# Moving a norm into a product and giving a 17th pair of columns to the seven-product scheme, in a hybrid decoder block

## The chip, the cores and the metric

The kernel runs on one core of a Trainium2 chip. The metric is the device time of one execution in microseconds (us). The core's engines are named as in the profile: PE (matrix products; PEld is its weight load), DVE (elementwise work), ACT (activations and copies), POOL and SP. POOL and SP do little here but issue DMA transfers.

## The reference, cut to what matters

The block adds 16 meta tokens to 512 tokens of width 1024, mixes them with two recurrent mixers and an output projection, and then applies a gated feed-forward part. The change touches the end of the output projection and the feed-forward part:

```
h = h + conv_glu_ffn(rmsnorm(h, norm2_w[l]), ffn_w_up[l], ffn_conv_w[l],
                     ffn_conv_b[l], ffn_w_down[l])

def conv_glu_ffn(h, w_up, conv_w, conv_b, w_down):
    u = causal_dwconv(h @ w_up, conv_w, conv_b)      # width 2 * 2816, 3 taps
    gate, val = jnp.split(u, 2, axis=-1)
    return (jax.nn.silu(gate) * val) @ w_down
```

Here rmsnorm multiplies each token by the reciprocal root of its mean square and each channel by norm2_w. A factor per token may be applied before or behind a product over the channels.

## The kernel before, in words

Tokens lie along the free axis, channels along the 128 partitions. A product of f32 accuracy is made of three passes over rounded halves: weight high with data high, weight high with data low, weight low with data high. Each weight chunk of 128 x 1024 is therefore loaded as a raw tile (SP), rounded to a high half (ACT, L182) and subtracted to a low half (DVE, L183). Raw tiles, high halves and low halves have three buffers each, so a split waits until PE has finished with the chunk three places earlier.

The up projection has 22 pairs of column blocks, j (gate) and 22 + j (value). KINDS gives the way of each pair.

- U: a plain product with u2, which is h times norm2_w without the factor per token; the result is multiplied by the factor rstd2 behind the product (tile fr, L963), and then the three taps are added up (L929 on ACT, two L931 on DVE). 48 matmuls a block, 96 a pair.
- N: the same product with the normed tokens n, which hold the factor already. There is no fr, and the taps read the product's bank.
- W: seven products of half size in place of eight (function scheme). The weights of three chunks are w0, w2 and w1 with a half chunk s4; sums of weight blocks for them are made in device memory by accumulating transfers that POOL issues (weight_sums, L209 to L217, in four groups, the last one gated by xr5 near the end of the output projection). The tokens are n and four sums t1 to t4 of quarter blocks of n. 84 matmuls a pair. Each pair also copies a partial result from one bank to another on ACT (L989) and takes s4 through a tile of its own (SP, then s4h on ACT, s4l on DVE).

The first five pairs of the up projection are U. In their time n and t are made, two of eight steps behind each pair: an even step of normed_tokens makes two n (L902) with their halves (L189, L190), an odd one the sums t with theirs (L912 to L915). Then come 16 W pairs and one N pair, and then the down projection, whose inputs ac (products of gate and value) have to be split as well; SPLITS says behind which pair each ac is split.

rstd2 is made by second_norm: two products of ones with the sum of squares (tiles psn2), a logarithm on ACT (L140) and an exponential (L141). ACT loads a table of functions where the next function is not in the one it holds.

The order on each engine is set when the program is built: a planner places the instructions of all engines by priorities and its own model of time, and issue_after ties an instruction behind another. Each engine, and the SP queue, then works strictly in that order. What stands behind a waiting instruction waits with it.

Of the kernel before, what the change touches and what calls it, by code (L numbers as in the profile page):

```python
# [10 lines left out]
AF = mybir.ActivationFunctionType  # L11
ALU = mybir.AluOpType
# [7 lines left out]
T0 = META - 2  # L20
NB = 4
DM = 1024
KD = DM // P
# [24 lines left out]

KINDS = "UUUUUWWWWWWWWWWWWWWWWN"
STEPS = {0: (0, 1), 1: (2, 3), 2: (4, 5), 3: (6, 7)}
SPLITS = {7: (0,), 8: (1, 2), 10: (3,), 13: (4,), 15: (5,), 18: (6,), 20: (7, 8), 21: range(9, 22)}
WS = [j for j in range(KF) if KINDS[j] == "W"]
GROUPS = WS[0:4], WS[4:8], WS[8:12], WS[12:]
HT = 258
# [6 lines left out]
def tile_block(ctx: ExitStack, tc: tile.TileContext, xT, w_in, w_dt, w_out, w_up, w_down,  # L63
               par, consts, consti, out, dbg=None):
    nc = tc.nc
    V, A, G, PE = nc.vector, nc.scalar, nc.gpsimd, nc.tensor
# [9 lines left out]
    def slot(name, n=NT, dtype=F32, parts=P, tag="m"):  # L76
        return gp.tile([parts, n], dtype, tag=tag, name=name, bufs=TAGS[tag])
# [35 lines left out]
    LOGS = "natural_log_exp_and_others"  # L113
# [78 lines left out]
    def weight_sums(js, behind):  # L192

        n = GROUPS.index(js)
        V.tensor_copy(ticks[:, n:n + 1], behind[:, T0:T0 + 1])
        gate = G.tensor_copy(tick[:], ticks[:, n:n + 1])
        halves = w_up.rearrange("(a j) p c -> j p a c", a=2)
        ds = {}
        for j in js:
            t = dp.tile([P, 4 * HK], F32, name=f"sums{j}")  # L200
            sumd[j] = t
            ds[j] = t[:].rearrange("p (n c) -> p n c", n=4)

        def twice(ap):
            return ap.unsqueeze(1).broadcast_to([P, 2, HK])

        with tc.issue_after(gate.ins):
            for j in js:
                G.dma_start(ds[j][:, 0:2], halves[j][:, :, 0:HK])  # L209
                G.dma_start(ds[j][:, 2:4], w_up[j].rearrange("p (n c) -> p n c", n=2))  # L210
            for j in js:
                G.dma_start(ds[j][:, 0:2], twice(w_up[KF + j][:, HK:]), accum_op=ALU.add)
                G.dma_start(ds[j][:, 2], w_up[KF + j][:, 0:HK], accum_op=ALU.add)
            for j in js:
                G.dma_start(ds[j][:, 0], w_up[KF + j][:, 0:HK], accum_op=ALU.add)
            for j in js:
                G.dma_start(ds[j][:, 3], ds[j][:, 0], accum_op=ALU.add)  # L217
# [42 lines left out]
        ahead(used[0] + 2)  # L260
        return wdone.pop(key)

    def product(groups, xh, xl, t0, nk, k0=0):


        for k in range(len(xh)):
            first, last = k0 + k == 0, k0 + k == nk - 1
            for ps, (hi, lo) in groups:
                wh, wl = hi[:, k * P:(k + 1) * P], lo[:, k * P:(k + 1) * P]
                for w, x, s, e in ((wh, xh[k], first, False), (wh, xl[k], False, False), (wl, xh[k], False, last)):  # L270
                    for a0, a1 in ((t0, HALF), (HALF, NT)):
                        PE.matmul(ps[:, O + a0:O + a1], w, x[:, a0:a1], start=s, stop=e)  # L272
# [29 lines left out]
    with first(190000):  # L302
# [3 lines left out]
        acc = None  # L306
# [538 lines left out]
    for j, s in oorder:  # L845
        w = weights("out", j, s)
        if s:
            pos[j] = banks2(f"pout{j}")
            product([(pos[j], w)], obh, obl, T0, 2 * KD)
            continue  # L850
        product([(pos[j], w)], oah, oal, T0, 2 * KD, KD)
        xr = slot(f"xr{j}", tag="y")
        nc.scalar.dma_start(xr[:, T0:], xT[:, j, T0:])
        V.tensor_tensor(xr[:, T0:], xr[:, T0:], pos[j][:, O + T0:O + NT], ALU.add)
        dump(f"h{j}", xr[:])
        hs.append(xr)
        if j == 5:
            weight_sums(GROUPS[3], xr)
        hi, lo = slot(f"u2h{j}", dtype=F32R, tag="u"), slot(f"u2l{j}", dtype=F32R, tag="u")
        A.activation(hi[:, T0:], xr[:, T0:], AF.Copy, scale=col(C_N2 + j))  # L860
        V.scalar_tensor_tensor(lo[:, T0:], xr[:, T0:], col(C_N2 + j), hi[:, T0:].bitcast(F32),
                               ALU.mult, ALU.subtract)
        u2h.append(hi)
        u2l.append(lo)
        sq = slot(f"hsq{j}", tag="pr")
        A.activation(sq[:, T0:], xr[:, T0:], AF.Square)
        if acc is None:
            acc = sq
        else:
            V.tensor_tensor(acc[:, T0:], acc[:, T0:], sq[:, T0:], ALU.add)  # L870
    rstd2 = slot("rstd2", tag="rs")

    u1 = []
# [75 lines left out]
    def conv3(j, kind):  # L949
        w = weights("up", j)  # L950
        ps = product_banks(False)[0]
        if kind == "U":
            product([(ps, w)], u2h, u2l, T0, KD)
        else:
            product([(ps, w)], nh, nl, T0, KD)
        if j == 0:
            second_norm()
        r = ps[:, O + T0:O + NT]
        c = slot(f"fc{j}", 512, tag="pr")
        with evac():  # L960
            if kind == "U":
                t = slot(f"fr{j}", tag="pr")
                V.tensor_tensor(t[:, T0:], r, rstd2[:, T0:], ALU.mult)  # L963
                r = t[:, T0:]
            taps(c[:], r, j, taps_of(j), col(C_FB + j))
        return c
# [214 lines left out]
```

## Time and profile before

| | |
|---|---|
| time, median of 3 runs | 872.89 us (872.69 to 874.68) |
| the profiled execution's own time | 873.16 us |
| span of its profile | 871.3 us |
| matmuls and DMA as the page counts them | PE x6746, 135.00 MB moved by DMA |
| output projection | to 501 us |
| five U pairs | 501 to 559 us |
| 16 W pairs | 559 to 728 us |
| N pair and down projection | to 862 us |

The three runs lie within 0.23% of each other. The profile's times count from the start of the span. The stage borders are read from PE's rows. Line numbers in the text are those of the kernel before; in the changed one, what stands from L272 on is two to five lines further down.

### The profile page before, as it was taken

How to read it: one execution, taken by the hardware profiler on the slowest of the kernel's cores; microseconds unless marked ns; L12 is line 12 of the kernel's file. 1: busy time of each engine (PE TensorE's matmuls, PEld its weight loads, DVE VectorE, ACT ScalarE, POOL GpSimd, SP SyncE). 2: the span in 40 equal slices, each digit the busy share in tenths (PEclk: the TensorE clock that was granted, in tenths of full speed). 3: DMA queues.
4: the chain of work that ended last, by engine and by line, in shares of the span. 5: the costliest groups of instructions: out<-in, count | busy, mean ns of one | idle time of the engine just before them, and what ended most of it. 6: DMA issues, size and time to landing. Idle time of an engine off the chain costs nothing.

```text
span 871.3 us, 16400 instructions
## 1 busy us (share of the span) xinstructions
PE 851.0 (98%) x6746; PEld 810.3 (93%) x6746; DVE 579.6 (67%) x970; ACT 464.1 (53%) x736; POOL 93.7 (11%) x130
## 2 busy tenths in 40 slices
PE   6999999999999999999999999999999999999995
PEld 6999899999999999999999999889999999888885
DVE  6984978799776766545333359978888886633233
ACT  8638975966445434454222265567666665533231
POOL 1000000003213221202221312100000000000001
PEclk9999999999999999999999999999999999999998
DMA  7234242213989598948998889756555553243312
GB/s 248 93 109 163 78 145 62 76 58 128 240 153 166 208 228 160 180 128 305 222 179 178 279 163 192 178 166 185 182 173 189 177 176 115 68 126 90 91 43 97
DMA packets 51867, 135.00 MB, mean 155 GB/s; under 512 B 5432, under 2 KB 9016, under 8 KB 51792
## 3 DMA queue, kind: packets, MB, share of 16 engines
q1 hardware_dynamic: 33392, 92.60, 33.1%
q0 software_dynamic: 15872, 37.75, 23.1%
q10 hardware_dynamic: 2528, 3.60, 1.3%
q8 instruction: 53, 0.87, 0.4%
q14 instruction: 22, 0.18, 0.1%
HBM read 131.78 MB, written 39.90 MB: 197 GB/s over the span
## 4 chain that ended last, share of the span: by engine, by line
PE 87%; DVE 6%; DMA 2%; ACT 2%; issue 1%; SPq 0%; DVEq 0%; ACTq 0%
PE pj L272 32%; PE pout L272 10%; PE pdn L1054 4%; PE pdn L1055 4%; PE pdn L1053 4%; PE pup L982 3%; PE pup L984 3%; PE pup L983 3%; PE psn L983 2%; PE psn L984 2%; PE psn L982 2%; PE pup L272 1%; DVE fc L931 1%; PE pdn L1068 1%; PE pdn L1067 1%
## 5 line engine op out<-in xcount | busy, mean ns | idle before, releaser
L272 PE MATMUL pj<-u_lo,whi_in 128*128 128x272 f32 (+1 forms) x752 | 156.5, 288 | 0.0
L272 PE MATMUL pj<-u_hi,wlo_in 128*128 128x272 f32 (+1 forms) x752 | 156.1, 286 | 0.0
L272 PE MATMUL pj<-u_hi,whi_in 128*128 128x272 f32 (+1 forms) x752 | 155.3, 287 | 0.0
L272 PEld LDWEIGHTS pj<-u_lo,whi_in 128*128 128x128 f32 x752 | 116.1, 188 | 2.4 <-issue 1.9
L272 PEld LDWEIGHTS pj<-u_hi,wlo_in 128*128 128x128 f32 x752 | 116.4, 189 | 2.0 <-issue 1.9
L272 PEld LDWEIGHTS pj<-u_hi,whi_in 128*128 128x128 f32 x752 | 115.6, 188 | 2.4 <-issue 2.3
L183 DVE TENSOR_TENSOR wlo_in<-raw_in,whi_in 128x1024 fp32r<-128x1024 f32 (+1 forms) x58 | 64.3, 1109 | 55.1 <-ACT whi_in L182 55.0
L182 ACT ACTIVATE whi_in<-raw_in 128x1024 fp32r<-128x1024 f32 (+1 forms) x58 | 56.1, 966 | 64.5 <-PE pj L272 59.2
L182 ACT ACTIVATE whi_w<-raw_w 128x1024 fp32r<-128x1024 f32 x48 | 50.7, 1056 | 22.8 <-PE pup L983 11.5
L183 DVE TENSOR_TENSOR wlo_dn<-raw_dn,whi_dn 128x1024 fp32r<-128x1024 f32 (+1 forms) x24 | 27.2, 1135 | 53.3 <-ACT whi_dn L182 53.3
L183 DVE TENSOR_TENSOR wlo_w<-raw_w,whi_w 128x1024 fp32r<-128x1024 f32 x48 | 58.6, 1221 | 5.5 <-ACT whi_w L182 5.0
L182 ACT ACTIVATE whi_dn<-raw_dn 128x1024 fp32r<-128x1024 f32 (+1 forms) x24 | 23.6, 989 | 69.2 <-PE pdn L1054 53.6
L1054 PE MATMUL pdn<-ac_lo,whi_dn 128*128 128x512 f32 (+1 forms) x154 | 55.9, 363 | 0.0
L1053 PE MATMUL pdn<-ac_hi,whi_dn 128*128 128x512 f32 (+1 forms) x154 | 55.7, 362 | 0.0
L1055 PE MATMUL pdn<-ac_hi,wlo_dn 128*128 128x512 f32 (+1 forms) x154 | 55.6, 361 | 0.0
L182 ACT ACTIVATE whi_out<-raw_out 128x1024 fp32r<-128x1024 f32 x16 | 17.0, 1061 | 55.6 <-PE pout L272 29.9
L183 DVE TENSOR_TENSOR wlo_out<-raw_out,whi_out 128x1024 fp32r<-128x1024 f32 x16 | 19.6, 1226 | 29.8 <-ACT whi_out L182 29.8
L1111 POOL TENSOR_TENSOR ot<-xr,rs 128x256 f32<-128x256 f32 x4 | 3.7, 944 | 311.0 <-ACT rs L1102 311.0
L982 PE MATMUL pup<-n_hi,whi_w 128*128 128x258 f32 x128 | 36.3, 283 | 0.5 <-ACT n_hi L189 0.5
L983 PE MATMUL psn<-t,whi_w 128*128 128x258 f32 x128 | 36.4, 284 | 0.0
L983 PE MATMUL pup<-n_lo,whi_w 128*128 128x258 f32 x128 | 36.2, 283 | 0.0
L982 PE MATMUL psn<-t,whi_w 128*128 128x258 f32 x128 | 36.1, 282 | 0.0
(371 smaller groups left out, 2364.2 us busy)
## 6 DMA issues: line engine op xcount, KB each, us to landing
raw_in<-in_w_in_dram SPq DMA_DIRECT2D x50, 512.0 KB, 5.0
sums<-in_w_up_dram POOLq DMA_DIRECT2D x48, 512.0 KB, 8.2
sums<-in_w_up_dram POOLq DMA_DIRECT2D x32, 256.0 KB, 8.3
raw_out<-in_w_out_dram SPq DMA_DIRECT2D x16, 512.0 KB, 6.7
raw_w<-in_w_up_dram SPq DMA_DIRECT2D x16, 512.0 KB, 3.5
raw_w<-sums SPq DMA_DIRECT2D x16, 512.0 KB, 4.1
raw_dn<-in_w_down_dram SPq DMA_DIRECT2D x16, 512.0 KB, 4.0
raw_up<-in_w_up_dram SPq DMA_DIRECT2D x12, 512.0 KB, 8.3
```

The source lines that it names most:

```text
L182: A.activation(hi[:, d], raw[:, d], AF.Copy)
L183: eng.tensor_tensor(lo[:, d], raw[:, d], hi[:, d].bitcast(F32), ALU.subtract)
L272: PE.matmul(ps[:, O + a0:O + a1], w, x[:, a0:a1], start=s, stop=e)
L931: V.scalar_tensor_tensor(c, at(s), w[2 - s], c, ALU.mult, ALU.add)
L982: PE.matmul(ps, wh, xh, start=first, stop=False, skip_group_check=True)
L983: PE.matmul(ps, wh, xl, start=False, stop=False, skip_group_check=True)
L984: PE.matmul(ps, wl, xh, start=False, stop=k == H - 1, skip_group_check=True)
L1053: PE.matmul(ps, wh, xh, start=k0 + k == 0, stop=False)
L1054: PE.matmul(ps, wh, xl, start=False, stop=False)
L1055: PE.matmul(ps, wl, xh, start=False, stop=k0 + k == KF - 1)
L1067: PE.matmul(ps[:], wh, ah[k0 + k][:], start=k0 + k == 0, stop=False)
L1068: PE.matmul(ps[:], wh, al[k0 + k][:], start=False, stop=False)
```

## The change

It has five parts.

1. The sum of squares is made ahead of the halves of u2 in the output projection, and the two psn2 products stand ahead of the last of the eight steps of the first gate product instead of behind that product.
2. The table that holds both logarithm and exponential is loaded once, behind the first square; the two loads at L140 and L141 go.
3. The first two steps of normed_tokens stand right behind the first gate product, and the others one pair earlier than before.
4. The fifth pair is N in place of U, so it uses n.
5. The 22nd pair is W in place of N. The fourth group of weight sums has five members instead of four, ac8 is split behind the last pair instead of behind pair 20, and there are 17 W pairs.

```diff
-KINDS = "UUUUUWWWWWWWWWWWWWWWWN"
-STEPS = {0: (0, 1), 1: (2, 3), 2: (4, 5), 3: (6, 7)}
-SPLITS = {7: (0,), 8: (1, 2), 10: (3,), 13: (4,), 15: (5,), 18: (6,), 20: (7, 8), 21: range(9, 22)}
+KINDS = "UUUUNWWWWWWWWWWWWWWWWW"
+STEPS = {0: (2, 3), 1: (4, 5), 2: (6, 7)}
+SPLITS = {7: (0,), 8: (1, 2), 10: (3,), 13: (4,), 15: (5,), 18: (6,), 20: (7,), 21: range(8, 22)}
...
-    def product(groups, xh, xl, t0, nk, k0=0):
+    def product(groups, xh, xl, t0, nk, k0=0, calls={}):
         for k in range(len(xh)):
+            if k in calls:
+                calls[k]()
...
+        sq = slot(f"hsq{j}", tag="pr")
+        square = A.activation(sq[:, T0:], xr[:, T0:], AF.Square)
+        if acc is None:
+            acc = sq
+            with tc.issue_after(square.ins):
+                A.preload_act_table_set(LOGS)
+        else:
+            V.tensor_tensor(acc[:, T0:], acc[:, T0:], sq[:, T0:], ALU.add)
         hi, lo = slot(f"u2h{j}", dtype=F32R, tag="u"), slot(f"u2l{j}", dtype=F32R, tag="u")
...
-        sq = slot(f"hsq{j}", tag="pr")
-        A.activation(sq[:, T0:], xr[:, T0:], AF.Square)
-        if acc is None:
-            acc = sq
-        else:
-            V.tensor_tensor(acc[:, T0:], acc[:, T0:], sq[:, T0:], ALU.add)
...
-            product([(ps, w)], u2h, u2l, T0, KD)
+            product([(ps, w)], u2h, u2l, T0, KD, calls={6: second_norm} if j == 0 else {})
...
         if j == 0:
-            second_norm()
+            for i in (0, 1):
+                normed_tokens(i)
```

The built programs differ from the output projection on. Three places matter below.

On ACT, where rstd2 is made. Before:

```order
L860 ACTIVATE u2h7_5985<-xr7_5982,pt_75 128x514
L866 ACTIVATE hsq7_5989<-xr7_5982 128x514
L182 ACTIVATE whi_up_23_6068<-raw_up_23_6067 128x1024
L140 ACT_TABLE_LOAD
L140 ACTIVATE rstd2_5992<-psn2_0_6053,eps_78 128x258
L140 ACTIVATE rstd2_5992<-psn2_1_6055,eps_78 128x256
L141 ACT_TABLE_LOAD
L141 ACTIVATE rstd2_5992<-rstd2_5992 128x514
```

Changed:

```order
L862 ACTIVATE hsq7_5993<-xr7_5990 128x514
L870 ACTIVATE u2h7_5996<-xr7_5990,pt_75 128x514
L140 ACTIVATE rstd2_6000<-psn2_0_6049,eps_78 128x258
L140 ACTIVATE rstd2_6000<-psn2_1_6051,eps_78 128x256
L141 ACTIVATE rstd2_6000<-rstd2_6000 128x514
L182 ACTIVATE whi_up_23_6106<-raw_up_23_6105 128x1024
```

Both loads are gone from here, and a weight half (whi_up_23) has moved from ahead of rstd2 to behind it.

On ACT again, at the N pair (pair 4), in the changed program:

```order
L182 ACTIVATE whi_w0_5_6627<-raw_w0_5_6626 128x1024
L933 ACTIVATE fc3_6557<-fr3_6558,pt_75 128x512
L189 ACTIVATE ac0_hi_7131<-ac0_6165 128x512
L189 ACTIVATE t4_2_6347<-t24_2_6333 128x258
L189 ACTIVATE n3_hi_6475<-n3_6473 128x514
L189 ACTIVATE n7_hi_6481<-n7_6479 128x514
```

n3_hi, which the N pair reads at its step 3, stands behind a weight half of the first W pair (pair 5). In the program before, n3 was not read until that W pair. Three rows further the changed program has:

```order
L189 ACTIVATE s4h_5_6759<-s4_5_6753 128x512
L1038 ACTIVATE fc3_6557<-fc3_6557 128x512
L189 ACTIVATE t2_3_6494<-t24_3_6486 128x258
L189 ACTIVATE t3_3_6497<-t13_3_6485 128x258
L182 ACTIVATE whi_w2_5_6686<-raw_w2_5_6685 128x1024
L933 ACTIVATE fc4_6680<-pup0_6011,pt_75 128x512
L189 ACTIVATE t4_3_6500<-t24_3_6486 128x258
L189 ACTIVATE s4h_6_6888<-s4_6_6882 128x512
L182 ACTIVATE whi_w1_5_6751<-raw_w1_5_6750 128x1024
```

Before, whi_w1_5 stood six rows ahead of s4h_5, and s4h_6 stood behind whi_w0_6; now both halves of s4, of pair 5 and of pair 6, stand ahead of whi_w1_5. On the SP queue the transfer of s4_5 now follows that of raw_w0_6 and s4_6 follows s4_5; before, s4_5 came behind raw_w2_6, and s4_6 three transfers later. On PE the first W pair begins, changed:

```order
L987 MATMUL p7_5_6745<-t3_0_6092,whi_w1_5_6751 128x258
L988 MATMUL p7_5_6745<-t3_0_6092,whi_w1_5_6751 128x258
L987 MATMUL pup0_6011<-n0_hi_6070,whi_w0_5_6627 128x258
L988 MATMUL pup0_6011<-n0_lo_6071,whi_w0_5_6627 128x258
L989 MATMUL pup0_6011<-n0_hi_6070,wlo_w0_5_6628 128x258
```

Two matmuls with w1 stand first now; before, nine matmuls with w0 stood ahead of them. In the N pair ahead of it PE alternates: 20 matmuls of the gate block, 20 of the value block (steps 0 to 2 and the high half of step 3), then 28 and 28.

On DVE, where the last pair ends and the down projection begins. Before:

```order
L190 TENSOR_TENSOR ac8_lo_8824<-ac8_7257,ac8_hi_8823 128x512
L931 SCALAR_TENSOR_TENSOR fc21_8881<-pup0_6003,pt_75,fc21_8881 128x512
L183 TENSOR_TENSOR wlo_dn_0_8_9004<-raw_dn_0_8_9002,whi_dn_0_8_9003 128x1024
L931 SCALAR_TENSOR_TENSOR fc43_8940<-pup1_6004,pt_75,fc43_8940 128x512 x2
L1036 TENSOR_TENSOR ac21_8944<-fc43_8940,fc21_8881 128x512
L190 TENSOR_TENSOR ac9_lo_8947<-ac9_7393,ac9_hi_8946 128x512
```

Changed:

```order
L1041 TENSOR_TENSOR ac21_8953<-fc43_8831,fc21_8830 128x512
L190 TENSOR_TENSOR ac8_lo_8956<-ac8_7261,ac8_hi_8955 128x512
L190 TENSOR_TENSOR ac9_lo_8960<-ac9_7397,ac9_hi_8959 128x512
L190 TENSOR_TENSOR ac17_lo_8992<-ac17_8433,ac17_hi_8991 128x512
L183 TENSOR_TENSOR wlo_dn_1_8_9023<-raw_dn_1_8_9021,whi_dn_1_8_9022 128x1024
L190 TENSOR_TENSOR ac10_lo_8964<-ac10_7525,ac10_hi_8963 128x512
L190 TENSOR_TENSOR ac18_lo_8996<-ac18_8561,ac18_hi_8995 128x512
L183 TENSOR_TENSOR wlo_dn_0_16_9077<-raw_dn_0_16_9075,whi_dn_0_16_9076 128x768
L190 TENSOR_TENSOR ac21_lo_9008<-ac21_8953,ac21_hi_9007 128x512
L190 TENSOR_TENSOR ac11_lo_8968<-ac11_7657,ac11_hi_8967 128x512
```

ac8_lo has moved behind ac21, the last result of the last pair. On PE, 20 matmuls of the down projection stand between the last matmul of that pair and the first that reads ac8 (ac8_hi), and ac8_lo is read by the next; before, 32 stood there.

## The prediction

> **What bounds the kernel now.** I read the page first, its shares and its chain.
>
> ```profile
> PE 851.0 (98%) x6746; PEld 810.3 (93%) x6746; DVE 579.6 (67%) x970; ACT 464.1 (53%) x736; POOL 93.7 (11%) x130
> PE 87%; DVE 6%; DMA 2%; ACT 2%; issue 1%; SPq 0%; DVEq 0%; ACTq 0%
> ```
>
> PE is the bound, so a microsecond is won only by fewer matmuls or by less idle time of PE. The second view, busy time by stretches, says where that idle time is in the part that changes (columns: length, then PE, PEld, DVE, ACT, POOL busy with instruction counts, granted clock, DMA share, GB/s).
>
> ```profile
> 540.00:560.00 20.00, 20.00 (x171) 19.95 (x169) 20.00 (x36) 10.61 (x19) 4.11 (x5) 1.00 0.98 217
> 560.00:571.00 11.00, 7.12 (x49) 6.06 (x48) 10.69 (x20) 7.24 (x15) 0.00 (x0) 1.00 0.30 83
> 571.00:720.00 149.00, 149.00 (x1241) 149.00 (x1241) 124.45 (x168) 102.43 (x153) 0.00 (x0) 1.00 0.58 183
> 720.00:760.00 40.00, 40.00 (x246) 35.74 (x245) 26.41 (x37) 20.96 (x32) 0.00 (x0) 1.00 0.31 93
> ```
>
> All of it lies between 560 and 571 us, at the first W pair. DVE is full there and before; PE is full everywhere else, through the turn to the down projection too, and the clock is full throughout. The third view, PE's timeline in that stretch, names the gaps (in brackets: idle before, and what ended it).
>
> ```profile
> 561.03 0.39 PE L982 MATMUL pup<-n_hi,whi_w 128*128 128x258 f32 x1 [0.53 <-ACT n_hi L189]
> 562.16 0.39 PE L984 MATMUL p<-t,wlo_w 128*128 128x258 f32 x1 [0.74 <-DVE wlo_w L183]
> 564.06 0.39 PE L1003 MATMUL pup<-n_hi,whi_w 128*128 128x258 f32 x1 [0.46 <-ACT psn L989]
> 567.98 0.39 PE L983 MATMUL p<-t,whi_w 128*128 128x258 f32 x1 [0.49 <-DVE t L190]
> 570.37 0.39 PE L982 MATMUL pup<-t,whi_w 128*128 128x258 f32 x1 [1.65 <-ACT pup L989]
> ```
>
> Together 3.87 us: this is all that an earlier start of n and t can win here. The last and longest is a transfer. In the chain and the timelines:
>
> ```profile
> 565.57 0.68 DVE L190 TENSOR_TENSOR s4l<-s,s4h 128x512 fp32r<-128x512 f32 x1
> 566.27 3.05 DMA s<-sums
> 569.41 0.63 ACT L189 ACTIVATE s4h<-s 128x512 fp32r<-128x512 f32 x1 [1.43 <-DMA s<-sums]
> ```
>
> s4 of pair 6 is fetched when DVE has done with s4 of pair 5; ACT stands still for it, and the copy behind it that PE wants (L989) comes late. This is the row to carry over to the new order.
>
> **The change part by part.** *One pair more by seven.* The sixteen executions of L1015, one a W pair, give its pace; the chain has a plain block of 48 matmuls.
>
> ```profile
> L1015 DVE TENSOR_TENSOR sv<-s,pup x16: 411/424/425, 572.2 to 724.0; 128x258 f32<-128x258 f32 x16
> 735.74 5.71 PE pup L272 x48
> ```
>
> A W pair takes (724.0 - 572.2) / 15 = 10.12 us, a plain pair 2 x 5.71 = 11.42. One of the plain pairs becomes W: **-1.30 us**.
>
> *The earlier rstd2.*
>
> ```profile
> 508.00 1.28 ACT L140 ACT_TABLE_LOAD   x1
> 510.15 1.28 ACT L141 ACT_TABLE_LOAD   x1
> 511.45 0.64 ACT L141 ACTIVATE rstd<-rstd 128x514 f32<-128x514 f32 x1
> 512.12 0.69 DVE L963 TENSOR_TENSOR fr<-pup,rstd 128x514 f32<-128x514 f32 x1 [2.87 <-ACT rstd L141]
> ```
>
> Two loads of 1.28 go, and psn2 stands 7 matmuls earlier on PE (7 x 5.71 / 48 = 0.83), so rstd2 is ready near 508.7 in place of 512.09. The one load left falls into the output projection, where ACT waits for PE. DVE starts some 3.5 us sooner, fills its waits before 520 with n0, n4 and t, and saves the two fr of the fifth pair (0.6 each). This feeds n and t; PE, full there, gains nothing by itself. I count all five gaps as removed, **-3.87 us**, and put beside it what is late in the new order.
>
> *The N pair wants n early.* It begins where the eighth plain block ends, which is where ACT now gets the buffer for the first half of w0:
>
> ```profile
> 547.46 1.06 ACT L182 ACTIVATE whi_w<-raw_w 128x1024 fp32r<-128x1024 f32 x1 [2.22 <-PE pup L272]
> 548.42 1.14 ACT L189 ACTIVATE n_hi<-n 128x514 fp32r<-128x514 f32 x2
> 549.78 0.80 ACT L929 ACTIVATE fc<-fr,pt 128x512 f32<-128x512 f32 x1
> 558.87 1.06 ACT L182 ACTIVATE whi_w<-raw_w 128x1024 fp32r<-128x1024 f32 x1 [0.87 <-PE pup L272]
> 559.84 0.61 ACT L189 ACTIVATE ac_hi<-ac 128x512 fp32r<-128x512 f32 x1
> ```
>
> PE reads n3_hi after 18 matmuls, 18 x 0.119 = 2.14 us later, at 549.60. ACT has whi_w0_5, fc3, ac0_hi and t4_2 ahead of it: 0.96 + 0.71 + 0.53 + 0.33 from start to start, and 0.62 for n3_hi itself: 547.46 + 3.15 = 550.61. PE waits **1.0 us**; 0 if ACT got n3 through sooner, 1.5 if DVE, full since 509, brings n3 half a microsecond late. The N pair ends near 559.9 (before, the tenth plain block ended at 558.87).
>
> *The first W pair wants w1 first, and ACT wants two s4 before that.* The transfers, their times to landing and the load on the DMA engines:
>
> ```profile
> 479.41 1.16 POOL L196 COPY tick<-ticks 128x1 f32<-128x1 f32 x1 [9.98 <-DVE ticks L195]
> 550.61 0.82 POOL L217 DMA_DIRECT2D sums<-sums  x1 [0.23 <-issue]
> 550.50 0.33 SPq L225 DMA_DIRECT2D raw_w<-in_w_up_dram  x1
> 556.16 0.42 SPq L232 DMA_DIRECT2D s<-sums  x1
> raw_w<-sums SPq DMA_DIRECT2D x1, 512.0 KB, 8.1
> s<-sums SPq DMA_DIRECT2D x16, 256.0 KB, 3.5
> raw_out<-in_w_out_dram SPq DMA_DIRECT2D x16, 512.0 KB, 6.7
> xr<-in_xT_dram ACTq DMA_DIRECT2D x8, 257.0 KB, 5.0
> 520.00:530.00 10.00, 10.00 (x86) 10.00 (x85) 10.00 (x19) 5.83 (x10) 2.04 (x2) 1.00 0.97 192
> ```
>
> POOL's fourth group of sums, four pairs, is issued from 479.4 to 551.4: 18 us a pair. A fifth member carries it to about 569. So the DMA share of 0.97 of 520 to 530, which before fell to 0.30 behind 560, now lasts through the start of the W pairs. Under it a load of 512 KB took 8.1 us (raw_w2_5, the only one issued between 540.5 and 541); in the output projection 512 KB took 6.7 and 257 KB 5.0 (medians); s4 itself, mostly in the empty stage, 3.5, and 3.05 above.
>
> Now the chain in the new order. raw_w0_6 goes out when DVE has finished wlo_w0_5, which waits for whi_w0_5: 547.46 + 1.06 + 1.22, so near 549.9, and s4_5 0.4 us behind it, at 550.3 (before: 556.16, wanted at 562.4). ACT reaches s4h_5 near 552. I let s4_5 land 7.2 us after its issue, at 557.5: 6.7 for the 512 KB issued just ahead, and something for its own 256 KB. Then s4h_5 (0.63) and s4l_5 (0.68) end at 558.85; that releases s4_6, as in the row above; it takes 5.0 under load and lands at 563.9. s4h_6 and whi_w1_5 behind it, 0.55 + 1.06, end at 565.5. PE has been waiting for whi_w1_5 since 559.9: **5.6 us**. Queued behind on ACT are the value taps of pair 4 and PE's first bank copy, which then meet a PE that is later than they are. Bounds: if both s4 land at 3.05, DVE's own row sum (DVE reaches s4l_5 near 555.5) lets s4_6 land at 559.3, and only whi_w1_5 itself, which cannot begin before PE releases its buffer at 559.9, is waited for: 1.1 us. If s4_5 takes 8.1 + 1.4 (256 KB at 192 GB/s) and s4_6 takes 8.1, PE waits until 570.9: 11.0 us. The nearest rows are those under load, so I take the middle.
>
> The Trainium skill, page "DMA: Bandwidth & Descriptors", section "Queues, rings and completion order", says that a DMA engine with work on several queues goes round them, some descriptors from each. By a fair half of 192 GB/s the 768 KB of raw_w0_6 and s4_5 would take about 8.2 us and the wait would be some 1 to 2 us longer, the sum as much higher. The 8.1 us for 512 KB agrees with sharing, at 65 GB/s; nothing here shows how two SP loads share.
>
> *Within the first W pair* one copy between banks stays on the path, as in the 0.46 gap: **+0.4 us**; 0 to 1.
>
> *The turn to the down projection.* Before, PE had two plain matmul runs and 32 down matmuls between its last up block and ac8. Now the last block's end E is followed by 20. The last pair's evacuation, with pair 20 as the model (its last matmul ended at E = 728.23):
>
> ```profile
> 728.27 0.78 ACT L929 ACTIVATE fc<-pup,pt 128x512 f32<-128x512 f32 x1 [1.89 <-PE pup L984]
> 731.96 0.69 DVE L1036 TENSOR_TENSOR ac<-fc,fc 128x512 f32<-128x512 f32 x1
> 745.71 4.90 DVE L190 TENSOR_TENSOR ac_lo<-ac,ac_hi 128x512 fp32r<-128x512 f32 x8
> 750.53 1.22 DVE L183 TENSOR_TENSOR wlo_dn<-raw_dn,whi_dn 128x1024 fp32r<-128x1024 f32 x1
> 733.04 0.39 PE L1069 MATMUL pdn<-ac_hi,wlo_dn 128*128 128x512 f32 x1
> 735.12 0.39 PE L1069 MATMUL pdn<-ac_hi,wlo_dn 128*128 128x512 f32 x1
> ```
>
> ac21 starts at E + 3.73. DVE goes on at 0.60 a half and 1.13 a weight chunk (0.88 for 768 columns): ac8_lo ends at E + 5.03, wlo_dn_1_8 at 7.37, ac11_lo at 10.65. PE's down matmuls come 0.231 apart (735.12 - 733.04 over nine); a matmul's row is longer than that step (0.39), so I let the first start 0.16 ahead of E: ac8_lo is wanted after 21 of them, E + 4.7; wlo_dn_1_8 after 29; ac11_lo after 40. Waits of 0.35, 0.5 and 0.75, each counted behind the one before: **1.6 us**, where before there was none. Bounds 0.5 and 2.5.
>
> *What costs nothing.* The other SP transfers of the last pair (three chunks for two) ride under 149 us of full PE at a DMA share of 0.58. sums21 is wanted only near 720. Squares ahead of u2 change no count.
>
> *Sum.* -1.30 - 3.87 + 1.0 + 5.6 + 0.4 + 1.6 = +3.4 us on 873.16, which lies 0.3 us over the median of 872.89: **876.6 us**, 0.4% over the median.
>
> **The rivals.** *The s4 loads land as in an empty stage*, because POOL's fifth member in fact leaves them room. Its late phases are small copies (256 KB at L215 and L217), which speaks for it; the share of 0.98 from 540 to 560, in just these phases, speaks against. Then the wait is 1.1 to 2 and the sum -1.30 - 3.87 + 1.0 + 1.5 + 0.4 + 1.6 = -0.7: 872.5, no change.
>
> *The order is forgiving throughout*: that, and DVE and ACT ahead enough that n3 and the splits at the turn come with little wait (0.2 and 0.5, and 0.2 inside the first W pair): -1.30 - 3.87 + 0.2 + 1.1 + 0.2 + 0.5 = -3.2: 870.0, faster. For it: the 3.87 us and the 12 matmuls are sure; against: the fixed orders on ACT and DVE, which put the late rows ahead of those that PE wants. It decides from a wait for whi_w1_5 under 1.2 us.
>
> *A transfer shared worse*: s4_5 and s4_6 at 8 us or more each, 11 in place of 5.6: 882.
>
> **How the numbers follow.** A difference under about 0.3% (2.6 us) cannot be told from none here. Chances: the forecast 0.48, empty-stage loads 0.25, forgiving 0.17, shared worse 0.10. The forecast's own range, waits of 3.5 to 8, is 874.5 to 879. Of the forecast's 0.48 some 0.06 falls within 0.3% (below 875.5), so slower 0.52; no change 0.31 (0.25 and 0.06); faster 0.17. For 8 in 10 the range goes from 870.0, into the forgiving case, to 880.5.
>
> **What would show it.** Right: a PE gap of 3 to 8 us ahead of the first matmul with w1 of pair 5, ended by ACT whi_w, behind an ACT wait on DMA s<-sums; sums transfers until about 569; a gap near 1 us in the N pair ended by n_hi; three waits on DVE at the turn; the five old gaps gone. Wrong: s landing in 3 us at 550 to 560, or PE through the N pair and the first W pair with under 2 us idle; then the time is 872 or less. PE's matmul count should fall by 12.

## The result, and the profile after

The changed kernel takes 879.45 us (median of 7 runs, 876.51 to 882.4); the kernel before took 874.68 beside it (7 runs, 872.69 to 876.33). The ratio is 1.0061, with a 95% interval from 1.0037 to 1.0085: slower by 0.6%. The forecast was 876.6, inside a range from 870.0 to 880.5. The profiled execution of the changed kernel took 876.51, with a span of 874.6; that is its fastest run, which matters further down.

The page, busy time and the shares of the chain, as shown of the kernel before:

```profile
PE 852.6 (97%) x6734; PEld 811.4 (93%) x6734; DVE 580.9 (66%) x972; ACT 464.8 (53%) x740; POOL 98.8 (11%) x136
PE 84%; issue 6%; DMA 3%; ACT 2%; DVE 2%; POOL 2%; SPq 0%; DVEq 0%; ACTq 0%; POOLq 0%
```

Twelve matmuls fewer, as forecast, and yet PE is busy for longer (852.6 against 851.0). PE's timeline, the rows with an idle stretch ahead of them:

```profile
551.04 0.74 PE L274 MATMUL pup<-n_hi,whi_up 128*128 128x258 f32 x4 [0.87 <-ACT n_hi L189]
564.25 0.58 PE L987 MATMUL p<-t,whi_w 128*128 128x258 f32 x1 [3.67 <-ACT whi_w L182]
573.50 0.39 PE L987 MATMUL pup<-t,whi_w 128*128 128x258 f32 x1 [0.28 <-ACT pup L994]
...
751.12 0.50 PE L1073 MATMUL pdn<-ac_lo,whi_dn 128*128 128x512 f32 x1 [0.23 <-DVE ac_lo L190]
753.46 0.50 PE L1074 MATMUL pdn<-ac_hi,wlo_dn 128*128 128x512 f32 x1 [0.22 <-DVE wlo_dn L183]
756.74 0.50 PE L1073 MATMUL pdn<-ac_lo,whi_dn 128*128 128x512 f32 x1 [0.49 <-DVE ac_lo L190]
```

The five old gaps are gone, and those that the prediction named have come in their place. The chain of waits shows the way to the gap of 3.67 us:

```profile
550.60 6.32 DMA s<-sums
557.00 0.64 ACT s4h L189
557.67 0.70 DVE s4l L190
558.39 4.15 DMA s<-sums
...
563.16 1.05 ACT whi_w L182
564.25 0.58 PE p L987
564.83 0.21 PE p L988
```

This is the forecast's chain: s4_5, its halves, s4_6, and whi_w1_5 behind them. The last row was not forecast: the matmuls behind it come 0.21 us apart, too, where the plain blocks take 0.119. The windows, cut where the granted clock changes (the column behind POOL's), say why:

```profile
559.86:563.28 3.42, 0.72 (x7) 0.51 (x5) 3.42 (x6) 1.50 (x4) 1.62 (x2) 1.00 0.97 173
563.28:566.69 3.41, 2.44 (x11) 2.44 (x12) 2.61 (x4) 2.10 (x3) 0.83 (x1) 0.50 0.91 133
566.69:570.10 3.41, 3.41 (x18) 3.41 (x17) 1.47 (x3) 0.66 (x2) 0.00 (x0) 0.50 1.07 266
570.10:573.52 3.42, 3.14 (x27) 2.93 (x26) 0.97 (x1) 1.53 (x3) 0.00 (x0) 1.00 0.67 210
```

After a stretch of 3.41 us in which PE was busy for 0.72, the clock is half for two such stretches, 18 matmuls in a full one, and 27 again in the shorter busy time of the last. That is why PE is busy for longer with fewer matmuls.

Two checkpoints divide the difference, without any reading of gaps: the sixteenth sum that ends a W pair, and the last down matmul ahead of the end. Of the kernel before, then of the change:

```profile
724.01 0.42 DVE L1015 TENSOR_TENSOR sv<-s,pup 128x258 f32<-128x258 f32 x1 [1.00 <-PE pup L984]
...
861.32 0.28 PE L1055 MATMUL pdn<-ac_hi,wlo_dn 128*128 128x256 f32 x1
```

```profile
726.91 0.42 DVE L1020 TENSOR_TENSOR sv<-s,pup 128x258 f32<-128x258 f32 x1 [0.76 <-PE pup L989]
...
864.81 0.28 PE L1060 MATMUL pdn<-ac_hi,wlo_dn 128*128 128x256 f32 x1
```

Up to the first the change loses 726.91 - 724.01 = 2.90 us, 0.35 of it ahead of the first gate matmul of the up projection (501.32 against 500.97). Behind the first, in the seventeenth pair and the turn, it loses (864.81 - 726.91) - (861.32 - 724.01) = 0.59. The sixteenth sum is not quite the same place in the two: counted from the first gate matmul, 1813 matmuls have started ahead of it before and 1811 in the change. A table further down, under the seventeenth pair, counts matmuls instead.

### The profile page after: what moved, and what is told of

It reads as the page before. It is cut to its first block, busy times and chain, and to the rows that moved or that the text cites. A ratio compares the mean times of both kernels' runs of the same rounds, so it can differ in the third digit from the quotient of the medians.

```text
span 874.6 us, 16411 instructions
## 1 busy us (share of the span) xinstructions
PE 852.6 (97%) x6734; PEld 811.4 (93%) x6734; DVE 580.9 (66%) x972; ACT 464.8 (53%) x740; POOL 98.8 (11%) x136
## 4 chain that ended last, share of the span: by engine, by line
PE 84%; issue 6%; DMA 3%; ACT 2%; DVE 2%; POOL 2%; SPq 0%; DVEq 0%; ACTq 0%; POOLq 0%
PE pj L274 32%; PE pout L274 8%; PE pup L987 4%; PE pup L989 4%; PE pup L988 4%; PE pdn L1059 4%; PE pdn L1060 4%; PE pdn L1058 3%; PE psn L988 2%; PE psn L989 2%; PE psn L987 2%; DMA s<-sums 1%; PE psy L574 1%; PE p L987 1%; PE p L988 1%
## 5 line engine op out<-in xcount | busy, mean ns | idle before, releaser
L183 DVE TENSOR_TENSOR wlo_w<-raw_w,whi_w 128x1024 fp32r<-128x1024 f32 x51 | 62.3, 1221 | 12.1 <-ACT whi_w L182 11.6
L182 ACT ACTIVATE whi_w<-raw_w 128x1024 fp32r<-128x1024 f32 x51 | 53.8, 1056 | 24.7 <-PE pup L988 13.1
L987 PE MATMUL pup<-n_hi,whi_w 128*128 128x258 f32 x136 | 39.1, 288 | 0.0
L988 PE MATMUL pup<-n_lo,whi_w 128*128 128x258 f32 x136 | 39.0, 287 | 0.0
L989 PE MATMUL pup<-n_hi,wlo_w 128*128 128x258 f32 x136 | 38.9, 286 | 0.0
L988 PE MATMUL psn<-t,whi_w 128*128 128x258 f32 x136 | 38.6, 284 | 0.0
L987 PE MATMUL psn<-t,whi_w 128*128 128x258 f32 x136 | 38.4, 282 | 0.0
```

The lines of the kernel that those rows point to most:

```text
L182: A.activation(hi[:, d], raw[:, d], AF.Copy)
L183: eng.tensor_tensor(lo[:, d], raw[:, d], hi[:, d].bitcast(F32), ALU.subtract)
L987: PE.matmul(ps, wh, xh, start=first, stop=False, skip_group_check=True)
L988: PE.matmul(ps, wh, xl, start=False, stop=False, skip_group_check=True)
L989: PE.matmul(ps, wl, xh, start=False, stop=k == H - 1, skip_group_check=True)
```

## The experiments

Theory A was by now: the gap is ACT's order (s4h_5 and s4h_6 ahead of whi_w1_5) together with late transfers, and the half clock follows from the gap. The rivals are in the expectations.

**s4 behind w1.** ACT and DVE take the halves of s4 behind the activation `whi` that makes whi_w1:

```diff
...
-        split_half(s4[:], h4[:], l4[:])
+        with tc.issue_after(whi.ins):
+            split_half(s4[:], h4[:], l4[:])
```

> The change with one thing undone in the order: ACT and DVE take the halves of s4 behind those of w1 of the same pair, so that whi_w1_5 waits for no transfer of s4. Theory A (the 3.67 us gap is the order on ACT, and the slow matmuls behind it follow from the gap's length): PE waits only for whi_w1_5 itself, about 1.1 us in place of 3.67; the granted clock from 560 to 571 stays at 1.00 in place of 0.69. That is 2.6 us less idle time and 2.7 us less slow matmuls: about 871.2 for a profiled execution (876.51 for the change, 873.16 before), a ratio to before of about 0.997. Rival B (late transfers: the gap only moves): PE waits for s4h_5 or s4h_6 instead, 2 to 4 us at the end of the first W pair or in the second, and the time stays near 876. Rival C (the half clock does not come from this gap): the gap falls to 1.1 us but the matmuls behind it still take 0.21 us each, about 873.9.

Measured: 870.83 us (870.46 to 871.47), ratio to before 0.9965 (0.9953 to 0.9977). Its timeline, PE and the sum at the first W pair's end:

```profile
561.64 0.39 PE L987 MATMUL p<-t,whi_w 128*128 128x258 f32 x1 [0.91 <-ACT whi_w L182]
568.32 0.39 PE L987 MATMUL pup<-t,whi_w 128*128 128x258 f32 x1 [0.29 <-ACT pup L994]
...
570.08 0.42 DVE L1020 TENSOR_TENSOR sv<-s,pup 128x258 f32<-128x258 f32 x1 [1.48 <-PE pup L989]
```

A wait of 0.91 us, no new one behind it, and the clock at 1.00 from 560 to 571: theory A, against B and C. The stretch from the first matmul with w1 to the first sum takes 570.08 - 561.64 = 8.44 us here. In the change its sum starts at 575.27, so the same stretch takes 575.27 - 564.25 = 11.02: the half clock costs **2.6 us**, beside the gap.

**The gap filled.** 26 matmuls whose results are overwritten stand where PE waits:

```diff
         seed(z, y)
+        if j == 5:
+            for _ in range(26):
+                PE.matmul(v, w2h[:, 0:P], b11[0][0], start=True, stop=True, skip_group_check=True)
         w1h, w1l, h4, l4 = weights("w1", j)
```

> The change with 26 matmuls more, whose results are overwritten, where PE waits for whi_w1_5: 26 x 0.119 = 3.1 us of work in a wait of 3.67. The transfers, ACT and DVE are as in the change. Theory A (the idle PE brings the half clock): the wait left is about 0.6 us, the granted clock from 560 to 571 stays at 1.00 and the matmuls behind it take 0.12 us; the end comes 2.7 us sooner than in the change, about 873.8 for a profiled execution. Rival C (the half clock has another cause, such as the load on the chip at that time): the matmuls behind still take 0.21 us and the time stays at 876.5. Rival D (the time from one run to the next, 876.5 to 882.4 in the change, comes from elsewhere): the runs spread as widely as those of the change.

Measured: 876.83 us (874.52 to 881.0, 12 runs), ratio 1.0042 (1.0025 to 1.0060). The profiled execution took 876.9:

```profile
561.17 3.36 PE L1015 MATMUL p<-n_hi,whi_w 128*128 128x258 f32 x26 [0.64 <-ACT whi_w L182]
567.33 0.39 PE L987 MATMUL p<-t,whi_w 128*128 128x258 f32 x1 [2.80 <-ACT whi_w L182]
```

The window of 3.41 us that holds most of the wait that was left, with the granted clock at 1.00:

```profile
562.91:566.32 3.41, 1.62 (x14) 1.41 (x12) 1.92 (x4) 0.61 (x2) 0.48 (x2) 1.00 1.02 140
```

The time that I had expected, 873.8, is missed, because the wait itself was longer: from 560.53 to 567.33, 6.8 us in place of 3.67, with the same order on ACT. The clock stayed full in this window and in those beside it, and the stretch behind it takes 8.44 us again (its first sum starts at 575.77), so in this execution the clock stayed up with the work in place. The window shown still had 1.79 us idle, and a window like that can go either way, as the run with gaps of chosen length shows further down. The timed runs spread as widely as those of the change (rival D), and the two ratios' intervals overlap, so they do not show what the filling is worth.

**The change once more.** Since the filled kernel's wait was so long, the change was profiled a second time.

> The change once more, for a second profile. Theory S (its wait hangs on when two shared transfers land, and so differs from one execution to the next, with the half clock behind it): a wait for whi_w1_5 between 3.5 and 7 us, one to three stretches of half clock, and a time that goes with them: 876.5 with 3.7 us, 879 to 882 with more. Rival (the difference between 876.5 and 882 comes from another part of the program): a wait near 3.7 us again and a time that differs.

It took 881.36. Its chain:

```profile
550.42 9.50 DMA s<-sums
...
561.39 5.90 DMA s<-sums
...
567.90 1.05 ACT whi_w L182
...
569.00 0.58 PE p L987
```

The same two transfers took 9.50 and 5.90 us where they had taken 6.32 and 4.15, and PE waited 8.59 us. The first matmul with w1 starts 569.00 - 564.25 = 4.75 us later, and the time is 4.85 longer: the difference between the two executions is this one wait (theory S, though the wait is longer than the 3.5 to 7 us given for it). The half clock behind it costs the same 2.6 (the first sum starts at 580.06, 11.06 behind).

**Four members in POOL's last group.** The last pair is plain again, so the fourth group of sums has four members, as before the change.

```diff
-KINDS = "UUUUNWWWWWWWWWWWWWWWWW"
+KINDS = "UUUUNWWWWWWWWWWWWWWWWN"
```

> The change with the last pair normed but plain (16 pairs by seven as before). POOL's fourth group of sums has four members again and should end near 551. Theory F (the fifth member of that group is the load that makes the two s4 late): s4_5, issued at 550.6, lands in 3 to 4 us and s4_6 in 3, PE waits 1.1 us for whi_w1_5, the clock stays full, and the three waits at the turn (0.94) go: 873.16 - 3.87 + 0.87 + 1.1 + 0.28 = 871.5. Rival G (SP's own 512 KB issued just ahead of s4_5, and what was still under way, make it late, with four members too): s4_5 still lands about 6 us after its issue, s4_6 in 3: a gap of 2.5 us and perhaps a low clock behind it, 873 to 876.

Measured: 874.58 us (872.29 to 877.16, 12 runs), ratio 1.0012 (1.0002 to 1.0022). The chain:

```profile
550.02 7.39 DMA s<-sums
557.50 0.64 ACT s4h L189
558.16 0.70 DVE s4l L190
558.88 3.03 DMA s<-sums
```

POOL issued its last sums at 548.83 here, and s4_5 is as late as ever: the fifth member is not what holds it up (theory F falls, and the figures are near rival G's). It holds up s4_6: 3.03 us without it, 4.15 and 5.90 with it. The wait in this profile is 3.64, with one stretch of half clock behind it.

**The sums finished earlier.** To see whether POOL's transfers are the load at all, with the change's order on ACT as it is:

```diff
-GROUPS = WS[0:4], WS[4:8], WS[8:12], WS[12:]
+GROUPS = WS[0:4], WS[4:9], WS[9:14], WS[14:]
```

> The change with POOL's sums grouped 4, 5, 5, 3 instead of 4, 4, 4, 5, so that the fourth group, which starts near 480, is issued by about 535 in place of 564.5; the order on ACT is the change's own (s4h_5 and s4h_6 ahead of whi_w1_5). With four members its last transfers still ran until 556, and s4_5 took 7 us. Theory L (POOL's transfers under way are what makes the two s4 late, whether the group has four members or five): s4_5, issued near 550.6, lands in 3 to 4 us, s4_6 goes out when DVE gets to s4l_5 and lands in about 3, PE waits about 1 us for whi_w1_5, the clock stays full: 871 to 871.5, as with s4 behind w1. Rival K (the 512 KB that SP issues 0.4 us ahead of s4_5 make it late): s4_5 still takes 6 us and more, the wait is 2.5 us or more: 873 to 876. A cost of the larger third group among the output gates' weights would show as gaps ahead of 500, up to 1 us.

Measured: 874.35 us (872.03 to 877.35, 11 runs), ratio 1.0012 (0.9997 to 1.0026). PE's timeline and, ahead of it, the third group's price:

```profile
394.66 0.50 PE L274 MATMUL pj<-u_hi,whi_in 128*128 128x258 f32 x2 [1.82 <-ACT sg L834]
...
564.75 0.39 PE L987 MATMUL p<-t,whi_w 128*128 128x258 f32 x1 [0.91 <-ACT whi_w L182]
```

```profile
392.16:395.57 3.41, 1.59 (x13) 1.39 (x12) 2.95 (x5) 1.56 (x3) 0.00 (x0) 1.00 0.64 197
395.57:398.99 3.42, 3.42 (x18) 3.42 (x17) 2.31 (x4) 1.14 (x2) 1.46 (x3) 0.50 0.23 76
```

POOL issued its last sum near 540. SP issued s4_5 at 553.86 and ACT had it at 557.73, 3.9 us later; s4_6 took 3.3; PE waited 0.91. So POOL's transfers under way are the load (theory L), and SP's own 512 KB, here too issued 0.4 us ahead, are not (K). From the first gate matmul to the last down matmul this run takes 358.16 us, the change 363.49. The time of the whole is 3 us over theory L's all the same: with the regrouping PE waited 1.82 us at 394.66, again with a stretch of half clock behind it, and the gate products began 3.3 us later than in the change. The regrouping came with that wait; by which link was not followed.

**How long a gap brings the half clock.** In the kernel before, seven of the copies of bank x to y were made several times over (pair 7 three times more, and so on), so that PE stands idle for chosen times:

```diff
...
-        seed(y, x)
+        seed(y, x, {7: 3, 9: 9, 11: 5, 13: 11, 15: 14, 17: 7, 19: 20}.get(j, 0))
```

> The kernel before, with the copy of bank x to y repeated in seven of its pairs by seven (3 times more in pair 7, 9 in 9, 5 in 11, 11 in 13, 14 in 15, 7 in 17, 20 in 19), so that PE stands idle there for about 0.9, 2.8, 1.5, 3.4, 4.3, 2.1 and 6.2 us; nothing else differs. Theory A (an idle stretch of some 3.5 us brings the half clock): after the gaps of up to 2.8 us the matmuls go on at 0.12 us each, after those of 4.3 and 6.2 at 0.21 for 3 us or more, and the one of 3.4 may do either. Rival C (the half clock behind the change's gap has another cause): no gap is followed by it. Rival H (short gaps do it as well): half clock from about 2 us on.

The gaps came out at 3.82, 1.78, 4.51, 5.80, 2.99 and 8.73 us (pairs 9 to 19 in order; that of pair 7 is too short to tell). Three of the places, in windows of 3.41 us: the old last gap, the gap of 1.78 and that of 4.51.

```profile
568.02:571.44 3.42, 1.74 (x13) 1.53 (x14) 2.61 (x4) 1.21 (x3) 0.00 (x0) 1.00 0.31 56
571.44:574.85 3.41, 3.41 (x19) 3.41 (x18) 1.65 (x2) 1.08 (x2) 0.00 (x0) 0.50 0.55 210
...
636.29:639.70 3.41, 1.62 (x14) 1.42 (x13) 3.02 (x5) 3.15 (x8) 0.00 (x0) 1.00 0.85 283
639.70:643.12 3.42, 3.42 (x19) 3.42 (x18) 1.95 (x4) 2.01 (x3) 0.00 (x0) 0.50 0.11 38
...
660.18:663.60 3.42, 1.62 (x14) 1.41 (x12) 2.37 (x4) 3.28 (x8) 0.00 (x0) 1.00 0.78 264
663.60:667.01 3.41, 0.70 (x5) 0.70 (x6) 1.80 (x3) 2.53 (x7) 0.00 (x0) 1.00 0.17 59
667.01:670.42 3.41, 3.41 (x18) 3.41 (x17) 0.80 (x1) 1.06 (x1) 0.00 (x0) 0.50 0.00 0
```

Rival H, and more: every one of these gaps is followed by half clock, that of 1.78 us too. Even the old last gap (the 1.65 of the prediction, 1.69 here) brought it on in this execution, and not in the profile before. The stretches of half clock lie on one grid of 3.41 us in each execution, and the rows go better with the idle time in a cell of that grid than with the length of a gap: 1.7 to 1.8 us idle may or may not bring it on (568.02 and 636.29 did, 660.18 did not), more than 2.2 did each time and under 1.3 never, in the profiles here.

**The splits earlier.** On top of s4 behind w1, the splits of ac8, ac9 and ac10 are made one pair sooner:

```diff
-SPLITS = {7: (0,), 8: (1, 2), 10: (3,), 13: (4,), 15: (5,), 18: (6,), 20: (7,), 21: range(8, 22)}
+SPLITS = {7: (0,), 8: (1, 2), 10: (3,), 13: (4,), 15: (5,), 18: (6,), 20: (7, 8, 9, 10), 21: range(11, 22)}
-    tag = ["z"] * 2 + ["bc", "u"] + ["fqv"] * 3 + ["ab"] * 2 + ["m"] * 8 + ["b0"] * 4 + ["b1"]
+    tag = ["z"] * 2 + ["bc", "u"] + ["fqv"] * 3 + ["ab"] + ["m"] * 8 + ["ab"] + ["b0"] * 4 + ["b1"]
```

> The run with s4's halves behind w1 (870.83 median), and beside it the splits of ac8, ac9 and ac10 made in pair 20 rather than in pair 21 (ac8 takes a buffer of another group for that, and ac16 takes its). Theory A (the three waits at the turn to the down projection are splits bunched behind the last pair): 0.22 + 0.21 + 0.44 = 0.87 us go, 870.0. Rival (DVE and ACT are then late somewhere else in pairs 20 and 21, since they have only so much room in a pair): the waits move and the time stays at 870.8.

Measured: 869.16 us (869.02 to 869.47), ratio 0.9948 (0.9935 to 0.9962): 1.7 us less. The three gaps are gone. The two checkpoints, of s4 behind w1 and of this run:

```profile
721.59 0.42 DVE L1020 TENSOR_TENSOR sv<-s,pup 128x258 f32<-128x258 f32 x1
...
859.42 0.28 PE L1060 MATMUL pdn<-ac_hi,wlo_dn 128*128 128x256 f32 x1
```

```profile
721.58 0.42 DVE L1020 TENSOR_TENSOR sv<-s,pup 128x258 f32<-128x258 f32 x1
...
857.45 0.28 PE L1060 MATMUL pdn<-ac_hi,wlo_dn 128*128 128x256 f32 x1
```

137.83 us against 135.87: from the seventeenth pair on the run is 1.96 shorter, twice the 0.87 that the three gaps show. Not all of that reaches the end. The run with early splits loses 0.93 in the second W pair (ACT stands still there for two late weight transfers, 2.44 and 0.87 us, and a copy between banks behind them comes late; a gap of 0.28 shows at 584.30), so from the first gate matmul to the last down matmul the two profiles differ by 357.94 - 356.92 = 1.02. Their first gate matmuls start 0.95 apart (501.48 and 500.53), which adds to the difference in time ahead of all that the edit is meant for.

**What the seventeenth pair is worth.** The same, with the last pair plain (the edit of KINDS above).

> The run with early splits (869.16 median), with the last pair normed but plain, so 16 pairs by seven. Theory (a pair by seven is worth the 1.30 us of the prediction's first term, once nothing waits for its splits or transfers): 870.5, 1.0 to 1.6 above the run with early splits. Rival (the seventeenth pair's gain is eaten by its own waits): within 0.4 of it.

Measured: 869.93 us (869.74 to 870.6), ratio 0.9962 (0.9949 to 0.9976): 0.77 above the run with early splits, between theory and rival. Its checkpoints:

```profile
721.39 0.42 DVE L1020 TENSOR_TENSOR sv<-s,pup 128x258 f32<-128x258 f32 x1 [0.54 <-PE pup L989]
...
858.05 0.28 PE L1060 MATMUL pdn<-ac_hi,wlo_dn 128*128 128x256 f32 x1
```

136.66 - 135.87 = 0.79, but this checkpoint hides part of it: with a plain last pair, four matmuls of that pair stand ahead of the sixteenth sum (1813 matmuls have started by then, 1809 with early splits), and 4 x 0.12 = 0.5 us. Counted from the same number of matmuls, in us:

| | first gate matmul to the 1805th matmul from it on | from there to the last down matmul |
|---|---|---|
| kernel before | 222.04 | 138.31 |
| change | 224.82 | 138.67 |
| change, last pair plain | 223.81 | 138.35 |
| s4 behind w1 | 219.60 | 138.34 |
| early splits | 220.53 | 136.39 |
| early splits, last pair plain | 219.59 | 137.66 |

So the pair is worth 137.66 - 136.39 = 1.27 us once nothing waits for its splits, as the theory has it; part of it does not show in the time, because of the two only the run with the seventeenth pair loses the 0.93 in the second W pair. With the change's own splits the pair does not pay: 138.67 with it against 138.35 without.

**The fifth pair plain.** First with the change's order on ACT, then on top of the early splits:

```diff
-KINDS = "UUUUNWWWWWWWWWWWWWWWWW"
+KINDS = "UUUUUWWWWWWWWWWWWWWWWW"
```

> The change with the fifth pair plain again instead of normed (17 pairs by seven, and the second norm early). Theory A: rstd2 is ready at 508.9 as in the change, so n and t are there in time, and ACT's row ahead of whi_w1_5 holds s4h_5 but not s4h_6: of the five old gaps (3.87 us) about 1.3 us are left ahead of the first matmul with w1 and 0.65 at a bank copy, the wait on n3_hi (0.87) goes away, the turn costs 0.94 as in the change, and the clock stays full: 873.16 - 1.30 - 3.87 + 1.95 + 0.94 = 870.9. Rival E (the early norm is not enough for n and t without a normed pair ahead of the W pairs): 3 us or more of gaps ended by n_hi and t remain from 558 to 571, and the time is 872.5 to 874. Rival B (late transfers set the gap whatever the order): a gap over 3 us ahead of w1, a low clock behind it, about 876.

Measured: 872.97 us (869.82 to 876.52, 12 runs), ratio 0.9988 (0.9976 to 1.0001). The profiled execution took 874.32 with a wait of 4.20 ahead of w1, as s4_5 took 10.19 us: rival B in this execution. Only s4h_5 stands ahead of whi_w1_5 here, so one late transfer is waited for and not two.

> As the run with early splits, and the fifth pair plain again instead of normed. Theory A (the order on ACT was all that made the fifth pair's norming necessary or harmful): the wait on n3_hi (0.87) goes, and that for whi_w1_5 (0.91) as well, as ACT can take it ahead of s4h_5; the copy between banks in the first W pair waits longer, up to 1.3 in place of 0.29. Sum -0.8 to -1.2: 868.8 to 869.2. Rival E (n and t come late without a normed pair ahead): gaps ended by n_hi or t of 1 us and more in the first W pair, 870 to 872.

Measured: 867.75 us (867.14 to 869.65), ratio 0.9935 (0.9923 to 0.9948), 1.4 below the run with early splits and the best of all. Neither n3_hi nor whi_w1_5 is waited for, and only the copy between banks is, for 1.09 us. Norming the fifth pair costs more than it brings.

**The second norm and the steps apart.** On s4 behind w1, the kernel's text has the norm's products behind the gate product again, and the early table load is taken out (the square stays ahead of u2):

```diff
-            with tc.issue_after(square.ins):
-                A.preload_act_table_set(LOGS)
...
-            product([(ps, w)], u2h, u2l, T0, KD, calls={6: second_norm} if j == 0 else {})
+            product([(ps, w)], u2h, u2l, T0, KD, calls={})
         if j == 0:
+            second_norm()
```

> The run with s4's halves behind w1 (870.83), with the second norm's products behind the first gate product again and both table loads at their old place. Theory N1 (the earlier rstd2 is what brings n and t in time): rstd2 is ready some 3 us later, n and t too, and waits ended by n_hi or t come up in the normed pair and the first W pair: 1 to 3 us more, 872 to 874. Theory N2 (DVE catches up before 549, and where n3_hi stands on ACT sets its time): no gap changes by more than 0.2 us and the time stays within 870.5 to 871.2.

Measured: 870.62 us (870.4 to 871.09), ratio 0.9965 (0.9952 to 0.9977), the same as with the norm early (theory N2). The test is weaker than I had meant. In the built program the two products did not move: they start 5.36 us behind the first gate matmul here and in the change (6.19 in the kernel before). The first table load is made ahead of them (at 503.16), and only the second, 1.28 us, is back in the chain. rstd2 was ready 8.85 us behind the first gate matmul, against 7.56 in the change, so 1.3 us later and not 3. Then, on the best run, the steps of n and t one pair later, with the norm early:

```diff
-STEPS = {0: (2, 3), 1: (4, 5), 2: (6, 7)}
+STEPS = {0: (0, 1), 1: (2, 3), 2: (4, 5), 3: (6, 7)}
-            for i in (0, 1):
+            for i in ():
```

> The run with early splits and the fifth pair plain (867.75 median), with the steps of n and t given out one pair later, as before the change; the second norm stays early. With the norm late in its place the run with s4 behind w1 kept its time, so rstd2's hour is not what removed the five old gaps. Theory P (the steps' place in the order is): gaps ended by n_hi, t and wlo_w come back between 558 and 571, 4 to 5 us more, 871.8 to 872.8. Rival (either of the two, the early norm or the early steps, is enough): no gap but the copy between banks (1.09), 867.5 to 868.3.

Measured: 874.97 us (872.16 to 877.09, 12 runs), ratio 1.0014 (1.0006 to 1.0023), 7.2 above it. PE's timeline:

```profile
561.15 0.39 PE L989 MATMUL p<-t,wlo_w 128*128 128x258 f32 x1 [0.40 <-DVE wlo_w L183]
562.43 0.39 PE L988 MATMUL pup<-n_lo,whi_w 128*128 128x258 f32 x1 [0.17 <-DVE n_lo L190]
563.39 0.38 PE L1008 MATMUL pup<-n_hi,whi_w 128*128 128x258 f32 x1 [0.46 <-ACT psn L994]
569.92 0.58 PE L987 MATMUL psn<-t,whi_w 128*128 128x258 f32 x1 [3.61 <-ACT t L189]
571.02 0.58 PE L988 MATMUL psn<-t,whi_w 128*128 128x258 f32 x1 [0.20 <-DVE t L190]
```

Five gaps of 4.84 us together are back, and half clock behind the longest (rows of 0.58). But they are not all of theory P's kind. On ACT, the halves of t stand behind s4h_5:

```profile
568.93 0.63 ACT L189 ACTIVATE s4h<-s 128x512 fp32r<-128x512 f32 x1 [5.05 <-DMA s<-sums]
```

s4_5 was issued at 561.50 and took 7.35 us, with POOL issuing its sums until 567.29, and ACT, then DVE's s4l, waited for it. The last two gaps (3.81 us) are therefore the late fetch again, in a new place in the order. The first three (1.03 us) are of the old kind, and the copy between banks among them (0.46) is waited for with the early steps too, for 1.09. So the early norm alone does not keep the waits for n and for the low half of w0 away, and the early steps do (theory P, in part); what the steps' place is worth without the fetch behind it, this run does not show.

## Why the prediction was right, and where it was not

It was right in direction and place: slower, through a wait for whi_w1_5 behind two fetches of s4. The sum of +3.4 us against the 876.51 - 873.16 = +3.35 of the two profiled executions owes its closeness to errors that cancel, and to luck: 876.51 is the fastest of seven. The median of 879.45 lies above the 874.5 to 879 that was given for the forecast itself. The two profiles of the change differ by their wait alone, so its median run waited for some 3.67 + (879.45 - 876.51) = 6.6 us, by my estimate.

- *The wait for whi_w1_5, +5.6.* The chain is the forecast's, row for row. Its transfers were given 7.2 and 5.0 us; they took 6.32 and 4.15 in one execution, 9.50 and 5.90 in the next, and the wait was 3.67 and 8.59, inside the bounds of 1.1 to 11.0. The reason was half wrong: POOL's transfers are the load (with the sums done early both land in under 4 us), but four members make s4_5 just as late (7.39); the fifth prolongs only s4_6 by 1 to 3 us.
- *The half clock, not in the sum.* I read "the clock is full throughout" off the kernel before and carried it over to an order with one long gap in place of five short ones. It costs 2.6 us. This is the step that failed: a term put at nothing.
- *The five old gaps, -3.87.* Their removal gave about 4.5. Up to the 1805th matmul the kernel before takes 222.04 us, and s4 behind w1, with gaps of 0.87, 0.91 and 0.29, takes 219.60; the difference of 2.44 and those 2.07 make 4.5. The rows of the prediction held the hint: 49 matmuls in 7.12 busy microseconds, 0.145 each against 0.119. Small waits hide in rows that count as busy.
- *What removes them.* I credited the earlier rstd2 as the feeder of n and t. With rstd2 1.3 us later no gap came back, and with the steps later two of the small ones did (0.40 and 0.17), so the runs speak for the steps' place; a norm as late as before, with the steps early, was not run. The last old gap (1.65) was a fetch of s4, and it went with the new order of the s4 rows.
- *One pair more by seven, -1.30, and the turn, +1.6.* Together +0.3 forecast and 138.67 - 138.31 = +0.36 measured, by the table. Apart, the pair brings 1.27, so the turn costs 0.36 + 1.27 = 1.63, of which the three gaps show 0.94. Both terms were right. (Early splits win more than 1.63 of the table's second column, since the kernel before loses 138.31 - 137.66 = 0.65 at its own turn.)
- *The N pair, +1.0, and the bank copy, +0.4:* 0.87 and 0.28 measured.
- *The rivals.* Transfers as in an empty stage did not come in the change (4.15 at the least). The forgiving order would have come with s4 behind w1: 870.83 measured, 870.0 forecast for it. The worse sharing (882) is near what the second profile shows, 881.36, so it is one end of this kernel's own spread, and 0.10 was too little for it; but its 11 us of wait were there 8.59 of wait and 2.6 of half clock. The rule of shared queues in the Trainium skill ("DMA: Bandwidth & Descriptors", "Queues, rings and completion order") would have made the wait 1 to 2 us longer; the transfers of the two executions lie on both sides of that.

With the clock added and the gaps at their true worth, the forecast's own terms give -1.27 - 4.5 + 0.87 + 3.67 + 2.6 + 0.28 + 1.63 = +3.3 for the profiled execution, from the first gate matmul to the last down matmul, where 363.49 - 360.35 = +3.14 was measured, and 4.9 more for the second.

## What to carry to other kernels

Before a late load is blamed, look at what stands behind it in the waiting engine's order: putting two copies behind one that PE wants first won 2.8 us of gap and 2.6 of clock, without a faster transfer. An idle stretch of TensorE has a second price, the slower matmuls behind it, so several short gaps can be cheaper than one long one. Measure a stretch by its count of matmuls, and not by the gaps alone; a fixed row of another engine can stand behind a different number of them in two kernels. Look in the built order whether an edit moved what it was meant to move.

## What was not expected of the hardware

- The clock is granted in cells of 3.41 us that lie on one grid per execution. Behind the first 12 us of each span, a cell at full clock with more than 2.2 us idle was followed by half clock in every profile here (the least was 2.24, steps late), one with less than 1.3 in none (the kernel before had 1.28 at 559.16), and 1.7 to 1.8 went both ways. The half clock lasted until a cell was busy nearly throughout: in the change it went on after the one with 2.44 us busy (563.28) and ended after the one with 3.41 (566.69); with gaps of chosen length it went on after 2.75 and ended after 2.98. The price was 1.6 us with one cell (last pair plain: its first sum starts at 573.66, 10.03 behind the matmul at 563.63, against 8.44) and 2.6 with two.
- The Trainium skill, page "TensorE: Matmul & The Clock Gate", Part 1, tells of a free-running window of 3413 ns and of half clock after an idle window. The grid agrees with these rows. A whole idle window is more than was needed here: a gap of 1.78 us was enough.
- A fetch of 256 KB behind POOL's adding transfers took 6.3 to 11.3 us in the profiles of the change and its variants (s4_5; the 11.3 with early splits, 6.3 and 9.5 in two executions of the same kernel), and 3.9 with those transfers done.
